# Softmax attention: the scores of the next two query tiles move from all five parts of a unit's output into its first two

## The chip, the cores and the metric

The kernel runs on one core of a Trainium2 chip. The metric is the device time of one execution in microseconds (µs). Its engines run side by side, each through its own list of instructions in order: TensorE (PE: matmuls; PEld: its weight loads), VectorE (DVE), ScalarE (ACT), GpSimd (POOL) and SyncE (SP, which issues transfers).

## The reference, cut to what matters

The whole kernel is a network of two blocks with two layers each; the change lies in the attention of its first layer. It has 6 query heads over 2 key heads, 1024 queries, and 256 + 1024 keys (a context and the sequence itself):

```python
def one_block(qblk):
    s = jnp.einsum('bqhgd,bkhd->bhgqk', qblk, k, preferred_element_type=jnp.float32) * scale
    p = jax.nn.softmax(s, axis=-1).astype(v.dtype)
    return jnp.einsum('bhgqk,bkhd->bqhgd', p, v)
...
y = jnp.concatenate([ya * jax.nn.silu(a_gate), yb * jax.nn.silu(b_gate)], axis=-1)
```

## The kernel before, in words

Every product of two fp32 operands is made of three matmuls of rounded parts (`mm3`, lines 202 to 204): a value x is split into a high part h and a low part l, and h·h, h·l, l·h are added up in PSUM. A split (`split`, lines 215 and 216) is a cast on ScalarE, which gives h, and a subtraction on VectorE, which gives l.

The attention (`ev_attn`) works in 24 **units**, numbered 0 to 23 here: head h = unit // 4, and in it pair pr = unit % 4 of two query tiles of 128 rows, **a** and **b**. What a unit needs is made in two generators.

`scores`, for each of the two tiles: matmuls into `pss` (6 of 512 columns, the sequence's keys; the pool has two such buffers) and into one half of `psc` (3 of 256 columns, the context's keys). Then the softmax: two maxima on VectorE (L602 over psc, L603 over pss), the bias from them (L604, L605), two exponentials on ScalarE with their sums (L608 gives `em`, L609 gives `ec`), and on VectorE the sum and its reciprocal (L610, L611). It has four steps: scores a, softmax a, scores b, softmax b.

`output`, in five parts. The weights of both tiles are transposed on TensorE in five **turns** T0 to T4 of four 128x128 blocks each (L627 into `pt`; T0 reads ec, T1 to T4 read em). Each turn is split into `pT`. Five **products** P0 to P4 of 6 matmuls (256 columns) add pT times the values up in `po`, where a small transpose also spreads the reciprocals (L649). Part 1 is T0 and T1; part 2 is L649, P0, T2; part 3 is P1; part 4 is T3, P2, T4, P3; part 5 is P4 and the gating on VectorE (L664, then L666 for heads 0 to 2, or L671 and one more split for heads 3 to 5).

The loop over units runs the `output` of unit n and, between its parts, the `scores` of unit n+1. At a unit's end `self.go()` now and then adds a piece of other work, the preparation of a later layer (**side work**, many small VectorE instructions, `s5_prep`).

This text is not the order on the engines. A scheduler takes it as a priority list, models when each instruction could start, and writes a fixed order for each engine; buffers are handed out on the way. An engine then executes its list in order and stops at the first instruction whose wait is not met. `pt`, `po` and `psc` share four buffers, `pss` has two.

Of the kernel before, what the change touches and what calls it, by code (L numbers as in the profile page):

```python
# [103 lines left out]
class Core:  # L104
# [468 lines left out]
    def ev_attn(self, ks, vs, scls):  # L573
# [5 lines left out]
        def head(h):  # L579
            qh, ql = self.tr("qh"), self.tr("ql")  # L580
            nc.sync.dma_start(qh.bitcast(F32), self.q_d[h, 0])
            nc.sync.dma_start(ql.bitcast(F32), self.q_d[h, 1])
            bg = self.t("bgl")
            nc.sync.dma_start(bg, self.bg_d[h])
            heads[h] = qh, ql, scls[h], bg

        def scores(h, pr, es):
            qh, ql, scl, _ = heads[h]
            kh, kl, kch, kcl = ks[h // 3]
            pc = self.psb("psc")  # L590
            for i in range(2):
                qt = 2 * pr + i
                qc = slice(qt * P, (qt + 1) * P)
                ps = self.psB("pss")
                cc = slice(i * CTX, (i + 1) * CTX)
                self.mm3(pc[:, cc], qh[:, qc], ql[:, qc], kch, kcl, True, True)
                for hv in HALVES:
                    self.mm3(ps[:, hv], qh[:, qc], ql[:, qc], kh[:, hv], kl[:, hv], True, True)
                yield
                st = self.s("st", [P, 8], "st", 6)  # L600
                sq = scl[:, qt:qt + 1]
                nc.vector.tensor_reduce(st[:, 1:2], pc[:, cc], axis=AX.X, op=ALU.max)  # L602
                nc.vector.tensor_reduce(st[:, 0:1], ps, axis=AX.X, op=ALU.max)  # L603
                nc.vector.tensor_scalar(st[:, 3:4], st[:, 0:1], st[:, 1:2], -1.0, op0=ALU.max, op1=ALU.mult)  # L604
                nc.vector.tensor_tensor(st[:, 3:4], st[:, 3:4], sq, op=ALU.mult)  # L605
                em = self.t("em")
                ec = self.s("ec", [P, CTX], "s1", 5)
                nc.scalar.activation(em, ps, AF.Exp, bias=st[:, 3:4], scale=sq, accum_out=st[:, 4:5])  # L608
                nc.scalar.activation(ec, pc[:, cc], AF.Exp, bias=st[:, 3:4], scale=sq, accum_out=st[:, 5:6])  # L609
                nc.vector.tensor_tensor(st[:, 6:7], st[:, 4:5], st[:, 5:6], op=ALU.add)  # L610
                nc.vector.reciprocal(st[:, 7:8], st[:, 6:7])  # L611
                es.append((ec, em, st))
                yield

        def output(h, pr, es):
            dc = slice((h // 3) * P, (h // 3 + 1) * P)
            pts = {}

            def weights_t(g):
                pt = self.psb("pt")  # L620
                for j in range(2):
                    kt = 2 * g + j
                    for i in range(2):
                        ec, em, _ = es[i]
                        src = ec[:, kt * P:(kt + 1) * P] if kt < 2 else em[:, (kt - 2) * P:(kt - 1) * P]
                        o = (2 * j + i) * P
                        nc.tensor.transpose(pt[:, o:o + P], src, self.ident)  # L627
                pT = self.tr("pT", (P, 2, HB))
                self.split(pt, pT[:, 0], pT[:, 1])
                pts[g] = pT  # L630

            def product(g):
                pT = pts.pop(g)
                for j in range(2):
                    kt = 2 * g + j
                    if kt < 2:
                        vh, vl = vC[:, 0, kt, dc], vC[:, 1, kt, dc]
                    else:
                        tt = kt - 2
                        vh, vl = vH[tt // 4][:, tt % 4, dc], vL[tt // 4][:, tt % 4, dc]  # L640
                    c2 = slice(j * CTX, (j + 1) * CTX)
                    self.mm3(po[:, :CTX], vh, vl, pT[:, 0, c2], pT[:, 1, c2], kt == 0, kt == 9)

            weights_t(0)
            weights_t(1)
            yield
            po = self.psb("po")
            for i in range(2):
                nc.tensor.matmul(po[:, CTX + i * P:CTX + i * P + P], es[i][2][:, 7:8].to_broadcast([P, P]), self.ident,  # L649
                                 start=True, stop=True)  # L650
            product(0)
            weights_t(2)
            yield
            product(1)
            yield
            weights_t(3)
            product(2)
            weights_t(4)
            product(3)
            yield  # L660
            product(4)
            cs = slice(pr * CTX, (pr + 1) * CTX)
            gate = self.s("gate", [P, CTX], "s1", 5)
            nc.vector.tensor_tensor(gate, po[:, CTX:], heads[h][3][:, cs], op=ALU.mult)  # L664
            if h < 3:
                nc.vector.tensor_tensor(y[2 + h][:, cs], po[:, :CTX], gate, op=ALU.mult)  # L666
                if pr == 3:
                    nc.gpsimd.dma_start(self.y_d[2 + h], y[2 + h])
            else:
                yo = self.s("yo", [P, CTX], "s1", 5)  # L670
                nc.vector.tensor_tensor(yo, po[:, :CTX], gate, op=ALU.mult)  # L671
                self.split(yo, y[2 + h][0][:, cs], y[2 + h][1][:, cs])
# [6 lines left out]
        for n, (h, pr) in enumerate(units):  # L679
            if pr == 0:  # L680
                y[2 + h] = self.t("yf") if h < 3 else (self.tr("yh"), self.tr("yl"))
            if pr == 2 and h < 5:
                head(h + 1)
            nxt = []
            sc = scores(*units[n + 1], nxt) if n + 1 < len(units) else iter(())
            o = output(h, pr, es)
            next(o)
            next(sc, None)
            next(o)
            next(sc, None)  # L690
            next(o)
            next(sc, None)
            next(o)
            next(sc, None)
            next(o, None)
            es = nxt
            self.go()
# [1520 lines left out]
```

## Time and profile before

| | |
|---|---|
| time, median of 3 runs | 4103.86 µs (4103.34 to 4109.02) |
| the profiled execution's own time | 4098.59 µs |
| its span (first to last instruction) | 4096.8 µs |
| PE, PEld, DVE, ACT busy over the span | 93%, 77%, 69%, 35% |
| attention: start of the first scores, start of the last gating (L671) | 533.5 and 817.7 µs |
| end of unit 0's first turns, about; start of unit 23's L664 | 546.70; 817.19 µs |
| mean from one L664 to the next | 11.3 µs |

The execution that was profiled took 4098.59 µs, 1.8 µs more than its span. The attention is one fourteenth of the span. "Busy" of PE counts from the start of a matmul to its modelled end; matmuls overlap, so a busy PE may still be short of work.

### The profile page before, as it was taken

The numbers are of one execution on the slowest core, as the hardware profiler recorded it, in microseconds if no ns is written. First come the engines' busy times: TensorE is split into PE (matmuls) and PEld (weight loads), VectorE is DVE, ScalarE is ACT, GpSimd is POOL, SyncE is SP. The second block draws the span as 40 slices with busy tenths as digits, with TensorE's granted clock in tenths as the row PEclk, the third lists the DMA queues.
The fourth block names the chain that finished last, engine by engine and source line by source line (L and its number), as shares of the span: only waits on it lengthen the run. The fifth ranks groups of instructions, "written<-read, shape, count | busy, mean of one in ns | idle before, by whom it ended". The sixth has DMA issues, their size and how long they took to land.

```text
span 4096.8 us, 51285 instructions
## 1 busy us (share of the span) xinstructions
PE 3816.4 (93%) x19684; PEld 3148.8 (77%) x19684; DVE 2842.5 (69%) x4892; ACT 1446.9 (35%) x2328; POOL 304.0 (7%) x533
## 2 busy tenths in 40 slices
PE   6899998899999996899999999989999899999997
PEld 3787887778788876687788888768787677888886
DVE  5676667785889787767866654457888867666544
ACT  3222245532112221434432333245555534232332
POOL 0001100041010022000000000010010000000000
PEclk9999999999999998999999999989999999999998
DMA  5434321163122348423322245333232333222542
GB/s 208 135 127 147 106 73 42 53 202 118 67 83 74 106 150 260 131 67 108 113 83 80 75 162 174 100 95 91 73 98 73 98 119 113 78 77 97 172 146 100
DMA packets 172907, 458.35 MB, mean 112 GB/s; under 512 B 38542, under 2 KB 59028, under 8 KB 172662
## 3 DMA queue, kind: packets, MB, share of 16 engines
q1 hardware_dynamic: 129254, 317.94, 23.5%
q0 software_dynamic: 41104, 132.41, 9.7%
q10 hardware_dynamic: 2304, 4.72, 0.3%
q8 instruction: 155, 2.54, 0.3%
q14 instruction: 90, 0.74, 0.1%
HBM read 327.07 MB, written 100.66 MB: 104 GB/s over the span
## 4 chain that ended last, share of the span: by engine, by line
PE 72%; DVE 11%; issue 4%; ACT 3%; DMA 2%; POOL 1%; SPq 1%; DVEq 0%; ACTq 0%; POOLq 0%
PE p L202 7%; PE p L203 7%; PE p L204 7%; PE pd L202 4%; PE pd L203 4%; PE pd L204 4%; PE pout L202 2%; PE pout L204 2%; PE pout L203 2%; PE pu L202 2%; PE pu L204 2%; PE pu L203 2%; DVE sbm L1946 2%; PE pwt L1967 1%; PE pz L1041 1%
## 5 line engine op out<-in xcount | busy, mean ns | idle before, releaser
L185 DVE TENSOR_TENSOR wl<-wt,wh 128x1024 fp32r<-128x1024 f32 x232 | 283.5, 1223 | 316.5 <-ACT wh L184 315.0
L184 ACT CAST wh<-wt 128x1024 fp32r<-128x1024 f32 x232 | 243.5, 1050 | 728.3 <-PE pd L203 218.6
L202 PE MATMUL p<-tq,wq 128*128 128x512 f32 x736 | 291.7, 396 | 3.5 <-ACT wq L215 3.5
L203 PE MATMUL p<-tq,wq 128*128 128x512 f32 x736 | 290.9, 395 | 0.0
L204 PE MATMUL p<-tq,wq 128*128 128x512 f32 x736 | 290.4, 395 | 0.0
L202 PE MATMUL pd<-hd,wh 128*128 128x512 f32 x704 | 278.7, 396 | 0.0
L203 PE MATMUL pd<-hd,wh 128*128 128x512 f32 x704 | 278.5, 396 | 0.0
L204 PE MATMUL pd<-hd,wl 128*128 128x512 f32 x704 | 278.3, 395 | 0.0
L204 PE MATMUL p<-hq,wq 128*128 128x512 f32 x480 | 189.9, 396 | 0.0
L203 PE MATMUL p<-hq,wq 128*128 128x512 f32 x480 | 189.6, 395 | 0.0
L202 PE MATMUL p<-hq,wq 128*128 128x512 f32 x480 | 189.5, 395 | 0.0
L215 ACT CAST wq<-ws 128x512 fp32r<-128x512 f32 x184 | 114.4, 623 | 209.5 <-PE p L204 204.9
L1717 DVE TENSOR_TENSOR fsg<-fsg,p 128x512 f32<-128x512 f32 x140 | 94.4, 686 | 117.9 <-PE p L204 117.9
L202 PEld LDWEIGHTS p<-tq,wq 128*128 128x128 f32 x736 | 138.1, 188 | 43.9 <-ACT wq L215 4.8
L204 PEld LDWEIGHTS p<-tq,wq 128*128 128x128 f32 x736 | 138.3, 188 | 33.1
L203 PEld LDWEIGHTS p<-tq,wq 128*128 128x128 f32 x736 | 138.3, 188 | 31.1
L1717 DVE TENSOR_TENSOR fsu<-fsu,p 128x512 f32<-128x512 f32 x140 | 94.5, 687 | 94.9 <-PE p L204 94.9
L216 DVE TENSOR_TENSOR wq<-ws,wq 128x512 fp32r<-128x512 f32 x184 | 126.7, 690 | 47.4 <-ACT wq L215 45.0
L204 PEld LDWEIGHTS pd<-hd,wl 128*128 128x128 f32 x704 | 132.3, 188 | 32.1
L202 PEld LDWEIGHTS pd<-hd,wh 128*128 128x128 f32 x704 | 132.2, 188 | 32.1
L203 PEld LDWEIGHTS pd<-hd,wh 128*128 128x128 f32 x704 | 132.2, 188 | 31.9
L202 PE MATMUL pu<-hq,wh 128*128 128x512 f32 x320 | 129.9, 406 | 9.4 <-DVE cv L978 9.4
(702 smaller groups left out, 10668.3 us busy)
## 6 DMA issues: line engine op xcount, KB each, us to landing
wt<-w_gu SPq DMA_DIRECT2D x88, 512.0 KB
wt<-w_dn SPq DMA_DIRECT2D x88, 512.0 KB
wm<-w_mod SPq DMA_DIRECT2D x48, 512.0 KB
hid<-fsg POOLq DMA_DIRECT2D x44, 512.0 KB, 3.9
hr<-hid SPq DMA_DIRECT2D x44, 512.0 KB
wt<-w_od SPq DMA_DIRECT2D x28, 512.0 KB
khat<-fX POOLq DMA_DIRECT2D x24, 512.0 KB, 3.0
kh<-khat SPq DMA_DIRECT2D x24, 512.0 KB
```

Source lines behind the costliest of these rows:

```text
L184: nc.scalar.copy(wh, wt)
L185: nc.vector.tensor_tensor(wl, wt, wh.bitcast(F32), op=ALU.subtract)
L202: mm(ps, lh, rh, start=first, stop=False)
L203: mm(ps, lh, rl, start=False, stop=False)
L204: mm(ps, ll, rh, start=False, stop=last)
L215: self.nc.scalar.copy(h, src)
L216: self.nc.vector.tensor_tensor(l, src, h.bitcast(F32), op=ALU.subtract)
L1041: mm(p4[:, i, q], tb[:, m], z[:, self.POS[m]], start=True, stop=False)
L1717: add = lambda o, u, v: tt(o, u, v, op=ALU.add)
L1946: nc.vector.tensor_tensor_scan(om[:, :n - 1], om[:, :n - 1], self.inv[:, 3:4].to_broadcast([P, n - 1]), 1.0, op0=ALU.mult, op1=ALU.add)
L1967: nc.tensor.transpose(pt[:, s * P:(s + 1) * P], W[x][:, c:c + P], self.ident)
```

## The change

Only the order in which the loop asks the two generators for their next step:

```diff
             sc = scores(*units[n + 1], nxt) if n + 1 < len(units) else iter(())
             o = output(h, pr, es)
+            next(sc, None)
             next(o)
+            next(sc, None)
             next(sc, None)
             next(o)
             next(sc, None)
             next(o)
-            next(sc, None)
             next(o)
-            next(sc, None)
             next(o, None)
             es = nxt
             self.go()
```

Before: part 1, scores a, part 2, softmax a, part 3, scores b, part 4, softmax b, part 5. Now: scores a, part 1, softmax a, scores b, part 2, softmax b, parts 3 to 5. No instruction is added or removed, but the scheduler is given another list, and the engines' orders differ from the start of the attention to its end (on PE, DVE and ACT; those of POOL and SP are the same). After the attention all orders are the same as before.

ScalarE, in the output of unit 4 (the casts of T0 to T4, and the exponentials of unit 5: em and ec of its tile a, then of b). Before:

```order
L215 CAST pT_4384<-pt_4379 128x512
L215 CAST pT_4392<-pt_4387 128x512
L215 CAST pT_4420<-pt_4415 128x512
L608 ACTIVATE em_4428,st_4423<-pss_4396,st_4423,qscl1_2472 128x1024
L609 ACTIVATE ec_4429,st_4423<-psc_4395,st_4423,qscl1_2472 128x256
L215 CAST pT_4455<-pt_4450 128x512
L215 CAST pT_4469<-pt_4464 128x512
L608 ACTIVATE em_4483,st_4478<-pss_4440,st_4478,qscl1_2472 128x1024
L609 ACTIVATE ec_4484,st_4478<-psc_4395,st_4478,qscl1_2472 128x256
```

Now, the same unit:

```order
L215 CAST pT_4395<-pt_4390 128x512
L215 CAST pT_4403<-pt_4398 128x512
L608 ACTIVATE em_4411,st_4406<-pss_4380,st_4406,qscl1_2472 128x1024
L609 ACTIVATE ec_4412,st_4406<-psc_4379,st_4406,qscl1_2472 128x256
L215 CAST pT_4441<-pt_4436 128x512
L608 ACTIVATE em_4449,st_4444<-pss_4417,st_4444,qscl1_2472 128x1024
L609 ACTIVATE ec_4450,st_4444<-psc_4379,st_4444,qscl1_2472 128x256
L215 CAST pT_4466<-pt_4461 128x512
L215 CAST pT_4480<-pt_4475 128x512
```

Tile b's exponentials stood behind the casts of T3 and T4, last in the unit; now they stand ahead of them, and tile a's stand ahead of the cast of T2.

VectorE, from the first subtraction of unit 4 (pT of T0, T1 and T2; st_4406 and st_4423 belong to unit 5's tile a, st_4444 to its tile b; yf is unit 3's gating). Before:

```order
L216 TENSOR_TENSOR pT_4384<-pt_4379,pT_4384 128x512
L216 TENSOR_TENSOR pT_4392<-pt_4387,pT_4392 128x512
L602 TENSOR_REDUCE st_4423<-psc_4395 128x1
L604 TENSOR_SCALAR st_4423<-st_4423 128x1
L605 TENSOR_TENSOR st_4423<-st_4423,qscl1_2472 128x1
L216 TENSOR_TENSOR pT_4420<-pt_4415,pT_4420 128x512
```

Now:

```order
L216 TENSOR_TENSOR pT_4395<-pt_4390,pT_4395 128x512
L666 TENSOR_TENSOR yf_3889<-po_4301,gate_4369 128x256
L216 TENSOR_TENSOR pT_4403<-pt_4398,pT_4403 128x512
L604 TENSOR_SCALAR st_4406<-st_4406 128x1
L605 TENSOR_TENSOR st_4406<-st_4406,qscl1_2472 128x1
L610 TENSOR_TENSOR st_4406<-st_4406 128x1
L611 RECIPROCAL st_4406<-st_4406 128x1
L216 TENSOR_TENSOR pT_4441<-pt_4436,pT_4441 128x512
L602 TENSOR_REDUCE st_4444<-psc_4379 128x1
L604 TENSOR_SCALAR st_4444<-st_4444 128x1
L605 TENSOR_TENSOR st_4444<-st_4444,qscl1_2472 128x1
L603 TENSOR_REDUCE st_4525<-pss_4499 128x1
```

L602 and L603 of tile a now come earlier (in the output of unit 3). Between the bias of tile a and that of tile b stand L610 and L611, which wait for tile a's exponentials, and the subtraction of T2.

TensorE, with what an instruction waits for, at the place where one unit's turns give way to the next. Before, the end of unit 4 and the turns T0 (pt_4498) and T1 (pt_4506) of unit 5, whose tile b is em_4483 and ec_4484:

```order
L627 MATMUL pt_4506<-ident_63,em_4428 128x128 [waits PE_49]
L203 MATMUL pss_4515<-kl_3378,qh_4128 128x512
L204 MATMUL pss_4515<-kh_3377,ql_4129 128x512
L627 MATMUL pt_4506<-ident_63,em_4483 128x128 [waits Activation_49]
L627 MATMUL pt_4506<-ident_63,em_4428 128x128
```

Now, in unit 4 behind turn T4 (pt_4475). pss_4499 and pss_4536 are the scores of unit 6, tiles a and b; pss_4536 takes the buffer of pss_4417, which em_4449 above reads:

```order
L627 MATMUL pt_4475<-ident_63,em_4285 128x128 [waits PE_49]
L627 MATMUL pt_4475<-ident_63,em_4323 128x128
L627 MATMUL pt_4475<-ident_63,em_4285 128x128
L627 MATMUL pt_4475<-ident_63,em_4323 128x128
L204 MATMUL pss_4499<-kh_3377,ql_4129 128x512
L202 MATMUL pss_4536<-kh_3377,qh_4128 128x512 [waits Activation_49]
L203 MATMUL pss_4536<-kl_3378,qh_4128 128x512
L204 MATMUL pss_4536<-kh_3377,ql_4129 128x512
L202 MATMUL psc_4498<-kc_916,qh_4128 128x256 [waits Activation_49]
L203 MATMUL psc_4498<-kc_916,qh_4128 128x256
L204 MATMUL psc_4498<-kc_916,ql_4129 128x256
L202 MATMUL po_4427<-pT_4466,vH_918 128x256 [waits Activation_49]
```

Before, the next unit's turns wait for the exponential of tile b. Now they have it long before, and it is the scores two units ahead that wait for it, with P3 and P4 of the running unit queued behind them.

## Rows read from the trace of the kernel before

**Rows 1.** Stretches from one L664 to the next: busy time by engine, granted clock, DMA.

```profile
core 0: us, PE busy (x) PEld busy (x) DVE busy (x) ACT busy (x) POOL busy (x), PEclk, DMA share, GB/s
...
632.06:645.91 13.85, 10.78 (x73) 9.14 (x72) 13.78 (x74) 6.44 (x16) 0.53 (x1) 1.00 0.25 100
...
667.11:678.00 10.89, 9.42 (x71) 8.84 (x71) 6.93 (x20) 7.16 (x14) 0.00 (x0) 1.00 0.29 84
...
723.79:739.15 15.36, 11.96 (x73) 10.43 (x72) 12.66 (x45) 5.66 (x14) 0.00 (x0) 0.89 0.27 100
...
771.57:786.65 15.08, 12.53 (x74) 10.42 (x72) 11.66 (x26) 5.53 (x14) 0.00 (x0) 0.89 0.00 1
...
808.39:817.19 8.80, 7.79 (x57) 6.77 (x57) 6.33 (x25) 4.27 (x10) 0.00 (x0) 1.00 0.72 270
817.19:826.00 8.81, 8.05 (x34) 5.92 (x33) 8.81 (x36) 5.15 (x6) 0.00 (x0) 1.00 0.61 231
sum 279.30, PE 254.27 PEld 222.91 DVE 216.91 ACT 156.41 POOL 1.60; mean PE 10.17 PEld 8.92 DVE 8.68 ACT 6.26 POOL 0.06
```

**Rows 2.** What TensorE's weight loads waited for, 533 to 820 µs: total, times, longest.

```profile
PEld pt L627 <- ACT em L608: 20.2, 18, 2.6
PEld pss L202 <- ACT em L608: 12.4, 8, 5.5
PEld po L203 <- DVE pT L216: 10.3, 23, 1.4
```

**Rows 3.** Timeline of TensorE in one unit: start, duration, instruction, idle before it.

```profile
659.66 0.60 PE L627 MATMUL pt<-ident,em 128*128 128x128 f32 x4
...
660.22 0.28 PE L203 MATMUL po<-pT,vH 128*128 128x256 f32 x1
...
661.67 0.39 PE L203 MATMUL po<-pT,vH 128*128 128x256 f32 x1
...
663.12 0.50 PE L202 MATMUL pss<-kh,qh 128*128 128x512 f32 x1 [0.16 <-ACT em L608]
...
663.69 0.40 PE L204 MATMUL pss<-kh,ql 128*128 128x512 f32 x1
663.93 0.28 PE L202 MATMUL psc<-kc,qh 128*128 128x256 f32 x1
664.04 0.28 PE L203 MATMUL psc<-kc,qh 128*128 128x256 f32 x1
...
668.58 0.55 PE L627 MATMUL pt<-ident,em 128*128 128x128 f32 x3 [1.79 <-ACT em L608]
```

**Rows 4.** Timeline of ScalarE in the same unit.

```profile
660.30 0.59 ACT L215 CAST pT<-pt 128x512 fp32r<-128x512 f32 x1 [2.03 <-PE pt L627]
...
662.97 0.56 ACT L609 ACTIVATE ec<-psc,st,qscl 128x256 f32<-128x256 f32 x1
...
663.51 1.07 ACT L215 CAST pT<-pt 128x512 fp32r<-128x512 f32 x2
667.23 1.21 ACT L608 ACTIVATE em<-pss,st,qscl 128x1024 f32<-128x1024 f32 x1 [2.65 <-DVE st L605]
```

**Rows 5.** Timeline of VectorE in the same unit.

```profile
658.00 1.28 DVE L216 TENSOR_TENSOR pT<-pt,pT 128x512 fp32r<-128x512 f32 x2
...
660.92 0.69 DVE L216 TENSOR_TENSOR pT<-pt,pT 128x512 fp32r<-128x512 f32 x1 [0.39 <-ACT pT L215]
...
663.65 0.16 DVE L610 TENSOR_TENSOR st<-st 128x1 f32<-128x1 f32 x1 [1.97 <-ACT ec L609]
...
665.33 0.41 DVE L602 TENSOR_REDUCE st<-psc 128x1 f32<-128x256 f32 x1
665.66 1.22 DVE L603 TENSOR_REDUCE st<-pss 128x1 f32<-128x1024 f32 x1
666.79 0.21 DVE L604 TENSOR_SCALAR st<-st 128x1 f32<-128x1 f32 x1
667.03 0.16 DVE L605 TENSOR_TENSOR st<-st,qscl 128x1 f32<-128x1 f32 x1
```

## The prediction

> **What bounds the kernel now.** I read the page first: PE is busy 93% of the span, and the attention is one stretch where it is less so. Then the stretches from one L664 to the next, which cut the attention into its units [rows 1]. From 546.70 µs, with the first turns of unit 0 done, to unit 23's L664 there are 279.30 − 8.81 = 270.49 µs for 24 units, 11.27 each. Three stretches, with much more VectorE work (13.78, 12.66 and 11.66 µs against 6.93 in a clean one), carry side work; they take 13.85, 15.36 and 15.08. The other 21 take (270.49 − 44.29) / 21 = 10.77 on average, so side work costs 44.29 − 3 × 10.77 = 12.0 µs. What does a unit's matmul work need? A turn takes 660.22 − 659.66 less one matmul, about 0.45; a 256-column matmul 0.12, a 512-column one 0.23 [rows 3]. Five turns (2.25), L649 (0.45), 30 + 6 matmuls of 256 (4.2) and 12 of 512 (2.8) make 9.7. So the units lie about 1 µs above their matmuls, and TensorE is not the only bound.
>
> The waits say what the rest is [rows 2]: turns wait for em, 20.2 µs in all, scores for em (their buffer) 12.4, products for the subtraction 10.3. And the timeline of one unit shows the loop: turn T2 at 659.66, its cast at 660.30, subtraction at 660.92, and so on through ScalarE and VectorE, em at 667.23, and the next turns at 668.58 after 1.79 of idling [rows 3 to 5]. One chain through three engines, not the matmuls, sets the unit.
>
> **The change, part by part.** No instruction comes or goes; SP and POOL have the same lists. So the sum is that of 24 units in the new orders, times the rows' durations. I take these steps from the rows: turn to cast 0.64 (659.66 to 660.30), cast 0.59, two in a row 1.07, subtraction 0.03 later, 0.69, the next 0.60 behind it; subtraction to product 0.06 (661.61 to 661.67); L602 0.41 and 0.33 to the next instruction, L603 1.22 and 1.13 to the next; L604 0.24, L605 0.20 until em starts; em 1.21, 0.14 until TensorE has its buffer (0.10 assumed after ec); ec to L610 0.68, ec to the next cast 0.54 [rows 3 to 5].
>
> *Removed.* The turns' wait for em (20.2 µs): b's exponentials now stand in the middle of the unit before, and T0 finds them done.
>
> *Added.* The lists of unit 4 (shown above) run like this, from its T0 at t = 0. Casts of T0, T1: 0.64 to 1.72. Subtraction T0 1.26 to 1.95; then yf, subtraction T1 from 2.2 to 2.9, and only then L604 at 2.80 and L605 for tile a: em a 3.24 to 4.45, ec a to 5.0. L610 and L611 wait for them (5.12, 5.32). Cast of T2 4.98 to 5.57, subtraction 5.60 to 6.29; only then L602 b at 6.2, L604, L605: em b 7.08 to 8.29, ec b to 8.84, casts of T3, T4 8.82 to 9.90. On TensorE: T0, T1 to 0.90; L649 takes T0's buffer and waits until 2.01; P0, T2, P1, T3 to 4.76; scores a (their buffer came free at 4.59), context scores b, P2 to 6.97; T4 and a's last matmul to 7.65. Here it stops: scores b of two units ahead need em b's buffer, so 8.43. Three matmuls, the context's, one of P3 and three more take it to 10.28, the rest of P3 and P4 to 11.57, where the next T0 starts. The unit takes **11.6 µs**, of which TensorE stands 1.9: 1.1 at L649, 0.8 at scores b.
>
> What is queued behind that last wait is P3, P4, the next T0 and with it the next round of the same chain: nothing hides it, since each engine's next link stands in order behind the one before. That is the cost of putting softmax b into the middle: its em sits ahead of the casts of T3 and T4, and its bias behind T2's subtraction.
>
> The other orders, by the same steps. **A**, as above: 9 units (2 to 4, 6 to 8, 10 to 12), 11.6 each. **C**: units 0, 1, 5, 9, where L604 and L605 of tile a stand ahead of T0's subtraction, so em a starts at 1.7 with the casts done; the scores of the next unit are not yet asked for at T3; 11.0 each. **A′**: units 15, 16, 19, 20 of heads 3 to 5, with the extra split of yo ahead of L604 a (em a 0.35 later) and L603 of the next tile a, 1.13, between L602 b and L604 b: em b 8.56 to 9.77, scores b at 9.91, 13.1 each. **B1**: 13, 17, 21, with ec a and the split of yo ahead of the casts of T0 and T1, so P0 gets its operand at 4.1, but the scores of tile b are left for the next unit: 11.1. **B2**: 14, 18, with both L603 in the chain and six 512-column matmuls ahead of L649: em a 4.43, em b 9.41 to 10.62, 13.9. Units 22 and 23, with less or no softmax left, 11.6 and as before 8.8 [rows 1].
>
> Sum: 9 × 11.6 + 4 × 11.0 + 4 × 13.1 + 3 × 11.1 + 2 × 13.9 + 11.6 + 8.8 = 282.3 µs. Side work comes on top. From below it is hidden: between L605 and L610 VectorE waits for two exponentials anyway (1.97 of idling in the row [rows 5]), and about half of the pieces stand there. From above it costs its 12.0 as before. I take 10, nearer to the upper end, since the other half stands ahead of an L604 or of a subtraction, in the chain. That makes 292.3 against 270.5: **+21.8 µs**, so 4098.6 + 21.8 = 4120.4 for an execution like the profiled one. The median of the runs shown lies 5.3 above that execution; on it the forecast is 4125.7. I say 4124.
>
> How far can the sum be off? Each order's chain has about 25 links; 0.4 µs per unit either way is 8.8 over 22 units, and side work from hidden to 12 adds −10 or +2. So +3 to +33 on top of 4098.6 to 4103.9: 4102 to 4137.
>
> **A rule on headroom.** By matmul busy time the units have 279.30 − 254.27 = 25 µs left, by weight loads 279.30 − 222.91 = 56 [rows 1]. The Trainium skill, "Trainium Kernel Development and Optimization", Best Practices, says that the distance to the limit is judged by weight loads, not by matmul busy time. By that the change would have up to 56 µs to win; but a 512-column matmul takes longer than its load, and the count above, 24 × 9.7 = 233, leaves 270.5 − 233 = 37.
>
> **Rivals.**
>
> *Faster: the wait at the turns simply goes.* For it: it is the largest wait [rows 2], and T0 no longer needs anything late. If the chain had slack, 20.2 µs of weight-load idling would go, up to 37 at the matmul bound: about 4080, and 4062 at most. Against it: T0's wait ends on a chain, and the new orders don't shorten that chain but close it elsewhere. It decides in this way if em b in A is done before TensorE comes to scores b, at 7.65: em b would have to start 0.8 earlier than 7.08.
>
> *No change: one wait for another.* If L604, L605 and the subtractions take less of VectorE than I count (0.8 µs per unit), the units come out at 10.8 to 11.3, as before: 4100 to 4108.
>
> *Slower still: the clock.* In the stretches with the longest waits (up to 5.5 µs [rows 2]) the granted clock is 0.89, in those with waits of 1.8 it is 1.00 [rows 1, 3]. If the 2.1 µs that A′ waits at scores b took the clock to 0.89 in A′ and B2, it would cost 0.11 × 13.5 × 6 = 9 µs more: 4135. The Trainium skill, "TensorE: Matmul & The Clock Gate", A second HAM failure mode, says that frequent short idling between matmul groups can make the clock go back and forth; the stretch at 667.11 with its 1.79 wait does not show that.
>
> **How the numbers follow.** Of no change a measurement of this kernel can tell about 0.2%, 8 µs. The chain as worked out (beyond +8): 0.74; the clock on top of it: 0.03; no change within 8: 0.13; faster: 0.10. So slower 0.77, same 0.13, faster 0.10. The likeliest case's own range is 4112 to 4140; taking in half of the case of no change, 4106 to 4140 holds 8 in 10.
>
> **What would show it.** In the profile after: turns waiting for em, 20.2 µs before, nearly nothing; the scores' wait for em 12.4 before, 20 to 40; L649 waiting for a subtraction, some 10 to 20. Casts of T3 after ec b, em a after the subtraction of T1. Stretches from L664 to L664 of 11.6 in units 2 to 7 with little scatter, 13 to 14 in the A′ and B2 units; the time up to 540 µs and from 830 µs on unchanged. It is wrong if stretches of A are at 10.5 or less, or if scores find their buffers free.

## The result, and the profile after

| | before | after |
|---|---|---|
| median of the runs | 4103.6 µs (4102.3 to 4109.02, 4 runs) | 4133.77 µs (4127.42 to 4134.88, 4 runs) |
| ratio, 95% interval | | 1.0069 (1.0055 to 1.0084) |
| the profiled execution (its span) | 4098.59 (4096.8) µs | 4127.42 (4125.6) µs |
| first to last L664 (units 0 to 23) | 259.76 µs | 285.42 µs |

The change makes the kernel 0.7% slower. Of the 28.8 µs between the two profiled executions, 25.5 are there at the last L664 (842.71 against 817.19 µs). Behind it the orders are the same and the distance wanders (the last L978, in the next layer, starts at 1357.3 against 1333.6, 23.7 later); executions of the kernel before alone lie up to 14.1 µs apart (4095.1 to 4109.24 in 13 runs). The remaining 3.3 µs are therefore not put down to the change.

The stretches from one L664 to the next, as in [rows 1]. The first is a unit of kind C, the second of kind A (kinds as in the prediction); then a B1 and a B2, an A′ with side work, the other B2, and unit 22:

```profile
core 0: us, PE busy (x) PEld busy (x) DVE busy (x) ACT busy (x) POOL busy (x), PEclk, DMA share, GB/s
557.29:568.22 10.93, 10.41 (x75) 9.20 (x74) 7.79 (x21) 6.18 (x13) 0.00 (x0) 1.00 0.16 53
...
591.44:603.14 11.70, 10.22 (x74) 9.16 (x73) 8.14 (x20) 6.20 (x13) 0.53 (x1) 1.00 0.11 46
...
697.47:707.49 10.02, 8.49 (x62) 7.59 (x61) 6.01 (x19) 6.41 (x14) 0.00 (x0) 1.00 0.01 2
707.49:722.48 14.99, 12.46 (x85) 11.04 (x84) 10.68 (x23) 6.50 (x14) 0.00 (x0) 1.00 0.00 1
...
735.51:752.86 17.35, 12.66 (x76) 10.89 (x75) 13.44 (x49) 6.50 (x14) 0.00 (x0) 0.90 0.26 92
...
762.89:779.25 16.36, 13.86 (x83) 12.25 (x82) 10.85 (x23) 6.50 (x14) 0.00 (x0) 0.90 0.00 1
...
820.29:834.98 14.69, 11.89 (x72) 10.45 (x71) 8.76 (x21) 7.08 (x15) 0.00 (x0) 0.83 0.10 31
```

Before, the stretches of units 1 to 12 without side work scattered between 8.23 and 12.09 µs; now the eight units of kind A without side work lie between 11.52 and 11.94. What TensorE's weight loads waited for in the attention (533 to 846 µs), as in [rows 2]:

```profile
PEld pss L202 <- ACT em L608: 31.1, 22, 4.9
PEld po L203 <- DVE pT L216: 12.4, 17, 2.6
PEld po L649 <- DVE pT L216: 12.1, 10, 1.3
...
PEld pt L627 <- ACT em L608: 0.4, 1, 0.4
```

The wait that the change takes away is gone (20.2 µs before, 0.4 now); the scores' wait for their buffer and a new one of L649 have taken its place. One unit of kind A, from its T0 at 591.05, shows how. VectorE, as in [rows 5]:

```profile
592.30 0.69 DVE L216 TENSOR_TENSOR pT<-pt,pT 128x512 fp32r<-128x512 f32 x1 [0.45 <-ACT pT L215]
592.91 0.41 DVE L666 TENSOR_TENSOR yf<-po,gate 128x256 f32<-128x256 f32 x1
593.24 0.68 DVE L216 TENSOR_TENSOR pT<-pt,pT 128x512 fp32r<-128x512 f32 x1
593.84 0.20 DVE L604 TENSOR_SCALAR st<-st 128x1 f32<-128x1 f32 x1
594.08 0.16 DVE L605 TENSOR_TENSOR st<-st,qscl 128x1 f32<-128x1 f32 x1
596.15 0.16 DVE L610 TENSOR_TENSOR st<-st 128x1 f32<-128x1 f32 x1 [1.91 <-ACT ec L609]
...
596.63 0.69 DVE L216 TENSOR_TENSOR pT<-pt,pT 128x512 fp32r<-128x512 f32 x1
597.23 0.42 DVE L602 TENSOR_REDUCE st<-psc 128x1 f32<-128x256 f32 x1
597.68 0.21 DVE L604 TENSOR_SCALAR st<-st 128x1 f32<-128x1 f32 x1
```

ScalarE, as in [rows 4]: em of tile a, the cast of T2, em of tile b, the casts of T3 and T4.

```profile
594.27 1.20 ACT L608 ACTIVATE em<-pss,st,qscl 128x1024 f32<-128x1024 f32 x1 [1.51 <-DVE st L605]
...
596.01 0.58 ACT L215 CAST pT<-pt 128x512 fp32r<-128x512 f32 x1
598.13 1.20 ACT L608 ACTIVATE em<-pss,st,qscl 128x1024 f32<-128x1024 f32 x1 [1.53 <-DVE st L605]
...
599.87 1.07 ACT L215 CAST pT<-pt 128x512 fp32r<-128x512 f32 x2
```

TensorE, as in [rows 3]: L649, the scores of tile b, the next unit's T0.

```profile
593.05 0.71 PE L649 MATMUL po<-ident,st 128*128 128x128 f32 x4 [0.96 <-DVE pT L216]
...
599.48 0.50 PE L202 MATMUL pss<-kh,qh 128*128 128x512 f32 x1 [0.52 <-ACT em L608]
...
602.74 0.60 PE L627 MATMUL pt<-ident,ec 128*128 128x128 f32 x4
```

Read together, these rows form one closed round. Tile a's bias stands behind the subtraction of T1, so em a starts 3.22 µs behind T0. The cast of T2 and L610 come only when tile a's exponentials are done; behind them come the subtraction of T2 and tile b's bias, and em b at 7.08. The scores follow at 8.43 and the next T0 at 11.69. TensorE stands only 1.5 µs in it, and still the unit is 0.9 longer than the average one without side work before. In the profile's own chain, the work that ended last followed back, this round stands whole in five of the nine units of kind A (2, 3, 6, 10 and 11). In the other four, the one shown among them, that chain runs over the subtraction of T0, L649, the matmuls and L603 of the next tile, or over the side work: a second path, of about the same length.

### The profile page after: what moved, and what is told of

It is laid out like the page before. It is cut to its first block, busy times and chain, and to the rows that moved or that the text cites. A ratio compares the mean times of both kernels' runs of the same rounds, so it can differ in the third digit from the quotient of the medians.

```text
span 4125.6 us, 51294 instructions
## 1 busy us (share of the span) xinstructions
PE 3821.3 (93%) x19684; PEld 3152.5 (76%) x19684; DVE 2842.1 (69%) x4892; ACT 1442.0 (35%) x2328; POOL 303.2 (7%) x533
## 4 chain that ended last, share of the span: by engine, by line
PE 76%; DVE 13%; issue 4%; ACT 3%; DMA 3%; POOL 1%; SPq 1%; DVEq 0%; ACTq 0%; POOLq 0%
PE p L202 7%; PE p L204 7%; PE p L203 7%; PE pd L202 4%; PE pd L204 4%; PE pd L203 4%; PE pout L202 2%; PE pout L204 2%; PE pout L203 2%; DVE sbm L1946 2%; PE pu L202 2%; PE pu L204 2%; PE pu L203 2%; PE pwt L1967 1%; PE pz L1041 1%
## 5 line engine op out<-in xcount | busy, mean ns | idle before, releaser
L202 PE MATMUL p<-tq,wq 128*128 128x512 f32 x736 | 292.3, 397 | 3.5 <-ACT wq L215 3.5
L203 PEld LDWEIGHTS p<-tq,wq 128*128 128x128 f32 x736 | 138.6, 188 | 31.1
L215 ACT CAST wq<-wt 128x512 fp32r<-128x512 f32 x138 | 85.3, 618 | 150.0 <-PE p L204 145.3
```

Source lines behind the costliest of these rows:

```text
L202: mm(ps, lh, rh, start=first, stop=False)
L203: mm(ps, lh, rl, start=False, stop=False)
L215: self.nc.scalar.copy(h, src)
```

## The experiments

Two theories. **The chain**: the fixed lists of VectorE and ScalarE close a round through em a, the cast and subtraction of T2, em b and the scores, and its length is the unit's. **The buffers**: the unit is long because the scores are asked for before one of their two buffers is free, which is where TensorE waits longest. "Stage" below is the time from the first L664 to the last in the profiled execution; the first L664 itself starts at 557.4 before and between 553.3 (runs 2 and 9) and 560.8 (runs 1 and 6) elsewhere, so up to 4 µs of a difference lie ahead of the stage. "Given high priority" means that the scheduler picks the instruction ahead of others that could start. The kernel before was run again beside each group: runs 1 to 4 are compared with its first median, 5 to 8 with the second, 9 with the third.

| kernel | stage, µs | median, µs (runs, or lowest to highest) | ratio to before, 95% |
|---|---|---|---|
| before | 259.76 | 4104.14 (25), 4101.84 (13), 4102.22 (9) | 1 |
| the change | 285.42 | 4133.77 (4) | 1.0069 (1.0055 to 1.0084) |
| 1: before, softmax b ahead of part 4 | 331.92 | 4176.75 (4171.62 to 4180.66) | 1.0181 (1.0166 to 1.0196) |
| 2: the change, softmax b last | 259.00 | 4095.80 (10) | 0.9988 (0.9979 to 0.9998) |
| 3: the change, bias first | 263.16 | 4101.60 (10) | 0.9995 (0.9986 to 1.0005) |
| 4: as 3, context scores together | 252.18 | 4095.72 (10) | 0.9983 (0.9974 to 0.9993) |
| 5: the change, context scores together | 277.53 | 4117.13 (6) | 1.0034 (1.0022 to 1.0046) |
| 6: the change, longer bias | 316.28 | 4149.70 (4) | 1.0119 (1.0102 to 1.0135) |
| 7: softmax b last, context scores together, maxima and bias first | 240.20 | 4076.12 (6) | 0.9936 (0.9923 to 0.9949) |
| 8: scores b behind part 2, context scores together, bias first | 243.28 | 4081.95 (6) | 0.9950 (0.9936 to 0.9963) |
| 9: before, context scores together, bias first | 237.35 | 4077.83 (5) | 0.9944 (0.9931 to 0.9958) |

**1. Only softmax b moved**, from behind part 4 to ahead of it; the scores stay where they were in the kernel before.

```diff
             next(o)
             next(sc, None)
-            next(o)
             next(sc, None)
+            next(o)
             next(o, None)
```

> The order before with one step moved: softmax b stands ahead of part 4 of the output, its scores stay where they were (output, scores a, output, softmax a, output, scores b, softmax b, output, output). Theory (one chain through the lists of ScalarE and VectorE): em b ahead of the casts of T3 and T4, and the two L603 in the chain; steps by the rows give 13 to 14 us per unit, so slower than the change itself: 4140 to 4165. Rival (the scores wait for their two buffers because they are asked for too early): the scores are late here and the turns no longer wait for em b, so the wait at the turns (20 us) goes and none takes its place: 4070 to 4095.

It is the slowest of all, beyond the chain's range and on the other side of before from that of the buffers. Two of its stretches from L664 to L664:

```profile
576.64:588.89 12.25, 10.84 (x75) 9.34 (x74) 8.46 (x21) 6.21 (x13) 0.00 (x0) 1.00 0.01 1
588.89:603.85 14.96, 11.95 (x73) 10.42 (x72) 8.25 (x20) 6.41 (x13) 0.00 (x0) 0.89 0.32 106
```

And the wait for the scores' buffer:

```profile
PEld pss L202 <- ACT em L608: 63.0, 32, 5.5
```

The scores are asked for late, and wait longer than in any other run: asking for them early is not what makes them wait. The chain's range left out the clock: 14 of the 23 stretches have a granted clock of 0.80 to 0.92, as the second row has, against 5 of 23 in the change. That this makes up the excess over the range is not shown.

**2. The change with softmax b put back to the end**: scores a and b and softmax a stay early.

```diff
             next(sc, None)
             next(o)
-            next(sc, None)
             next(o)
             next(o)
+            next(sc, None)
             next(o, None)
```

> The change with softmax b left at the end, between parts 4 and 5 (scores a, output, softmax a, scores b, output, output, output, softmax b, output). Theory (chain): the casts of T3 and T4 stand ahead of em b again; units alternate between some 10 and 13 us, mean 11.2 to 11.6 with side work: 4100 to 4118, most of the loss gone. Rival (buffers): both scores are asked for early and the buffers are held longer than in the change: 4130 or more.

All of the loss is gone, and a little more than the chain foresaw; with units of 11.4 and 10.7 µs in turn:

```profile
575.58:586.96 11.38, 11.18 (x76) 9.69 (x74) 9.17 (x21) 4.79 (x10) 0.00 (x0) 1.00 0.29 90
586.96:597.62 10.66, 9.71 (x70) 8.78 (x70) 7.10 (x19) 7.86 (x17) 0.53 (x1) 1.00 0.25 103
```

Yet the wait at the buffers is nearly that of the change:

```profile
PEld pss L202 <- ACT em L608: 26.9, 21, 4.9
```

(In every order one such wait, of 4.2 to 5.5 µs, lies ahead of unit 0's turns; it is in these sums.) What has gone instead are the waits of L649, 12.1 µs for subtractions of pT and 5.3 for the gating (L666 and L671) in the change and none here. So asking early for the scores costs nothing by itself. It is softmax b in the middle of the unit that costs, in the lists that come of it.

**3. The change with L604 and L605 given high priority**, for both tiles, so that tile a's bias stands ahead of the subtractions of T0 and T1, and tile b's ahead of that of T2.

```diff
-                nc.vector.tensor_scalar(st[:, 3:4], st[:, 0:1], st[:, 1:2], -1.0, op0=ALU.max, op1=ALU.mult)
-                nc.vector.tensor_tensor(st[:, 3:4], st[:, 3:4], sq, op=ALU.mult)
+                with self.tc.high_priority(): nc.vector.tensor_scalar(st[:, 3:4], st[:, 0:1], st[:, 1:2], -1.0, op0=ALU.max, op1=ALU.mult)
+                with self.tc.high_priority(): nc.vector.tensor_tensor(st[:, 3:4], st[:, 3:4], sq, op=ALU.mult)
```

> The change, with the bias of each tile (L604, L605) given high priority, so that on VectorE it stands ahead of the subtractions of T0 and T1 (tile a) or of T2 (tile b); ScalarE keeps the change's order. Theory (chain): em a starts at 1.7 instead of 3.2 us into the unit, as in the units of kind C: units of A at 10.8 to 11.1 instead of 11.65, those of heads 3 to 5 shorter by 0.5 to 1; 4112 to 4125. Rival (buffers): the scores are asked for at the same places, so as the change, 4127 to 4137.

```profile
587.05 0.20 DVE L604 TENSOR_SCALAR st<-st 128x1 f32<-128x1 f32 x1
...
587.50 0.15 DVE L605 TENSOR_TENSOR st<-st,qscl 128x1 f32<-128x1 f32 x1
587.73 0.69 DVE L216 TENSOR_TENSOR pT<-pt,pT 128x512 fp32r<-128x512 f32 x1
```

Em a now starts at 588.07, as soon as the casts of T0 and T1 are done, and the whole loss goes, with all steps of the change in place: more than the 4112 to 4125 that the chain promised. The orders moved elsewhere too. Units now take about 12.5 and 9.2 in turn, the long ones with more of the matmuls (PE busy 12.5 and 8.2), and in this short one em b starts 3.5 µs behind em a, at 591.55, where it was 3.9 in the unit of the change shown above. The wait at the buffers fell with the time, from 31.1 to this:

```profile
PEld pss L202 <- ACT em L608: 13.7, 7, 4.9
```

So this run refutes the time that the buffers forecast, but does not tell the two theories apart by the wait; run 2 does.

**4. As 3, and the context scores of both tiles asked for together with tile a's**, into the two halves of psc, so that L602 of tile b no longer waits for three matmuls behind ec a.

```diff
-                self.mm3(pc[:, cc], qh[:, qc], ql[:, qc], kch, kcl, True, True)
+                if i == 0: [self.mm3(pc[:, t * CTX:(t + 1) * CTX], qh[:, (qt + t) * P:(qt + t + 1) * P], ql[:, (qt + t) * P:(qt + t + 1) * P], kch, kcl, True, True) for t in range(2)]
```

> As e3, and the context scores of tile b (3 matmuls) are issued with those of tile a, so that they don't wait for ec a, which reads the same PSUM tile. Theory (chain): the link ec a, context scores b, L602 b goes too; em b starts soon after ec a: units of A at 10.1 to 10.6; 4098 to 4115. Rival (buffers): as the change, 4127 to 4137.

Another 6 µs, and a time just below before; the gain that the chain forecast was again too small.

**5. The context scores alone**, without priority (the diff of 4 on top of the change).

> The change, with the context scores of both tiles asked for together with tile a's (nine matmuls of 256 columns in a row into both halves of psc); no priorities. It takes one link out of the chain: L602 of tile b no longer waits until tile a's ec and three matmuls are done, and stands ahead of the subtraction of T2 instead of between it and L604 b. The bias of tile a still stands behind the subtraction of T1. Chain: em b comes about 0.4 us earlier in the units of kind A and A-prime, so 13 x 0.4 = 5 us less than the change, 4125 to 4132. Rival (it is the context link that makes the change slow, the place of tile a's bias costs nothing): most of the loss goes, 4100 to 4112.

Between the two forecasts. In the stage, units 1 to 12 gained nothing (140.71 µs from the first L664 to unit 12's, 140.18 in the change), against the 0.4 per unit expected; the 8 µs came from the units behind, most of them from those that are of kind A′ in the change (13.03 to 10.48 µs and 13.66 to 10.61 without side work). VectorE in a unit of kind A whose T0 is at 591.07 shows why:

```profile
596.24 0.42 DVE L602 TENSOR_REDUCE st<-psc 128x1 f32<-128x256 f32 x1
...
597.25 0.20 DVE L604 TENSOR_SCALAR st<-st 128x1 f32<-128x1 f32 x1
597.62 1.23 DVE L603 TENSOR_REDUCE st<-pss 128x1 f32<-128x1024 f32 x1 [0.17 <-PE pss L204]
598.76 0.15 DVE L605 TENSOR_TENSOR st<-st,qscl 128x1 f32<-128x1 f32 x1
```

L602 is a µs earlier than in the change, but the scheduler then put L603 of the next tile a, 1.23 µs, between the two instructions of tile b's bias: em b starts 7.88 µs behind T0 instead of 7.08.

**6. A longer bias**: in the change, L605's value is copied twice more on VectorE.

```diff
-                nc.vector.tensor_tensor(st[:, 3:4], st[:, 3:4], sq, op=ALU.mult)
+                nc.vector.tensor_tensor(st[:, 3:4], st[:, 3:4], sq, op=ALU.mult); nc.vector.tensor_scalar(st[:, 2:3], st[:, 3:4], 1.0, None, op0=ALU.mult); nc.vector.tensor_scalar(st[:, 3:4], st[:, 2:3], 1.0, None, op0=ALU.mult)
```

> The change, with two more small VectorE instructions in each tile's bias behind L605 (its value is copied twice, about 0.2 us each with the step to the next), so that em starts some 0.45 us later; the orders of ScalarE stay the same in the units of kind A. Chain: tile a's 0.45 and tile b's 0.45 both lie in the loop of a kind-A unit, since tile b's bias stands behind L610 and L611, which wait for tile a's exponentials: 0.5 to 0.9 more per unit, 22 units, 4145 to 4155. Rival (the bias has slack, and the units are long because TensorE is asked for the scores before their buffers are free or runs at a lower clock): 46 x 0.45 us of VectorE work lies in its idle time, 4130 to 4138.

The median is on the chain's side. The profiled execution is the slowest of the four (4159.47 µs, the others 4144.11 to 4154.78), and 8 of its 23 stretches have a granted clock of 0.78 to 0.90, against 5 in the change, so its stage overstates the loss; the unit read here has 1.00. It lost a µs more than I had expected, since the lists changed again. In the unit of kind A whose T0 is at 601.94:

```profile
608.50 0.42 DVE L602 TENSOR_REDUCE st<-psc 128x1 f32<-128x256 f32 x1
609.04 1.23 DVE L603 TENSOR_REDUCE st<-pss 128x1 f32<-128x1024 f32 x1
610.18 0.20 DVE L604 TENSOR_SCALAR st<-st 128x1 f32<-128x1 f32 x1
...
612.34 0.50 PE L202 MATMUL pss<-kh,qh 128*128 128x512 f32 x1 [2.30 <-ACT em L608]
```

L603 of the next tile a has come between L602 and L604 of tile b again, and L604 starts 1.68 µs behind L602, 0.45 in the change. So em a starts 3.60 µs behind T0 (0.38 later than in the change) and em b, at 610.99, 9.05 behind it: 1.97 later, of which the copies of both tiles make 0.76 and L603 1.23. The next T0 comes 13.66 behind this one, 11.69 in the change: 1.97 as well. All of em b's lateness is in this unit's length. In kind C (the unit from 616.01) em b is 1.6 µs later by the same comparison and the unit grew from 10.95 to 11.69: there the scores had their buffer before and wait 0.86 now, so half of the lateness was covered.

**7. Softmax b last as in 2, the context scores as in 4, and L602 to L605 given high priority** (beside the diffs of 2 to 4):

```diff
-                nc.vector.tensor_reduce(st[:, 1:2], pc[:, cc], axis=AX.X, op=ALU.max)
-                nc.vector.tensor_reduce(st[:, 0:1], ps, axis=AX.X, op=ALU.max)
+                with self.tc.high_priority(): nc.vector.tensor_reduce(st[:, 1:2], pc[:, cc], axis=AX.X, op=ALU.max)
+                with self.tc.high_priority(): nc.vector.tensor_reduce(st[:, 0:1], ps, axis=AX.X, op=ALU.max)
```

> Tile b's softmax asked for last in the unit, as in the second run of the study, with the context scores of both tiles together with tile a's, and L602 to L605 given high priority in the scheduler, so that the maxima and the bias stand ahead of the subtractions. Chain: the two exponentials lie half a unit apart, neither behind a subtraction; no turn and no scores wait for long, and a unit comes to 9.9 to 10.6 us instead of 11.3: 4075 to 4092, faster than before. Rival (the units are bound by something that these orders don't touch, buffers or the clock): as the two runs that it joins, 4093 to 4104.

In the chain's range, 0.6% faster than the kernel before and 1.4% faster than the change. The wait at the scores is down to 6.4 µs in four places, 4.3 of them ahead of unit 0. Two of its stretches:

```profile
573.60:583.98 10.38, 10.38 (x75) 9.58 (x74) 7.89 (x21) 6.36 (x13) 0.00 (x0) 1.00 0.34 99
583.98:593.51 9.53, 9.53 (x71) 8.90 (x70) 7.97 (x21) 6.33 (x13) 0.53 (x1) 1.00 0.28 115
```

TensorE is busy for the whole of each of these two: here the matmuls are the bound, close to the 9.7 per unit counted in the prediction.

**8. Scores b behind part 2**: the order scores a, part 1, softmax a, part 2, scores b, parts 3 and 4, softmax b, part 5, with the context scores as in 4 and the priority as in 3.

```diff
             next(o)
             next(sc, None)
-            next(sc, None)
             next(o)
             next(sc, None)
             next(o)
             next(o)
+            next(sc, None)
             next(o, None)
```

> The steps in the order scores a, part 1, softmax a, part 2, scores b, parts 3 and 4, softmax b, part 5 (tile b's scores behind part 2 instead of ahead of it), with the context scores of both tiles together with tile a's and L604 and L605 given high priority in the scheduler. Chain: as the run beside it, but tile b's scores are asked for only when their buffer is about to be free: units of 9.9 to 10.6, 4078 to 4094. Rival (bound by something that these orders don't touch): 4093 to 4104.

In the chain's range too.

**9. The kernel before, untouched in its steps, with the two edits of 4.**

> The kernel before, its steps in their own order (part 1, scores a, part 2, softmax a, part 3, scores b, part 4, softmax b, part 5), with the context scores of both tiles asked for together with tile a's, and L604 and L605 given high priority in the scheduler: what the two fastest runs share, without the change's earlier steps. Chain: L602 b no longer waits for three matmuls behind ec a, which takes some 0.4 us off in some units, but em b still stands behind the split of T3 and the next unit's T0 still waits for it: 4088 to 4100. Rival (the context scores and the priority alone made those runs fast, the order of the steps does not matter): 4072 to 4086.

The rival's time is right and my own forecast was wrong. Without any step moved it is as fast as 7. What TensorE's weight loads waited for:

```profile
PEld pss L202 <- ACT em L608: 9.9, 3, 5.2
...
PEld pt L627 <- ACT em L608: 5.0, 17, 0.6
```

The timeline of one unit, L605 of tile b, the subtraction of T3, and em b:

```profile
599.04 0.15 DVE L605 TENSOR_TENSOR st<-st,qscl 128x1 f32<-128x1 f32 x1
...
599.44 0.69 DVE L216 TENSOR_TENSOR pT<-pt,pT 128x512 fp32r<-128x512 f32 x1
...
600.33 1.22 ACT L608 ACTIVATE em<-pss,st,qscl 128x1024 f32<-128x1024 f32 x1
```

And the sum over its stretches from L664 to L664:

```profile
sum 237.35, PE 229.22 PEld 205.63 DVE 195.41 ACT 144.76 POOL 1.60; mean PE 9.97 PEld 8.94 DVE 8.50 ACT 6.29 POOL 0.07
```

I had taken it that em b's bias comes behind the split of T3, whatever the priority, as long as softmax b is asked for behind part 4. It now stands ahead of T3's subtraction, em b follows the cast of T4 without a wait (2.65 before [rows 4]), and starts 3.2 µs behind the cast of T2 (at 597.14) instead of 6.9 [rows 4]. So the turns wait 5.0 µs in all instead of 20.2. The two edits take 24 µs off the kernel before and 38 off the change (4133.77 to 4095.72); the change costs 30 µs without them and still 18 with them. So the order of the steps does matter: what the rival says of it holds for runs 7 to 9, not for run 4.

## Why the prediction was right

The sign and the mechanism were right. The size, 21.8 µs forecast between profiled executions and 28.8 measured, was a quarter too small, and 4133.77 lies 10 µs above the 4124 named. By its own steps:

- **Removed.** The turns' wait for em: 20.2 to 0.4, as said.
- **Kind A.** Of the steps worked out for it, L649 starts 2.00 µs behind T0 (forecast 2.01), em a at 3.22 (3.24), em b at 7.08 (7.08), scores b at 8.43 (8.43), the next T0 at 11.69 (11.57). Only the wait at scores b is 0.52 instead of 0.8, since one more 512-column matmul stands ahead of it than I counted. The eight units without side work sum up to 93.5 µs, forecast 92.8.
- **C, B1, A′.** The four C (unit 0 from 546.70) take 43.7, forecast 44.0. B1 and B2 are right only as a pair: 10.02 + 14.99 = 25.0 for units 13 and 14, forecast 11.1 + 13.9 = 25.0; L664 falls earlier than I drew it, so the sign of 13 to 14 µs for B2 missed (14.99 and 16.36). The two A′ without side work take 13.03 and 13.66, forecast 13.1.
- **Side work.** 17.35 − 13.1, twice, and 13.61 − 11.6: 10.5 in all, forecast 10. The clock is in it: both stretches of 17.35 have a granted clock of 0.90, as the two before had 0.89 [rows 1].
- **The term that was too small** is the stage: 842.71 − 546.70 = 296.0 against 292.3. Of the 3.7, 1.4 lie in units 17 and 18, 1.0 in 21 to 23, 0.6 in unit 19, 0.5 in side work; the rest is spread. The first of these is the clock, part of the rival that I had given 0.03: stretches of the same order without side work take 14.99 at a granted clock of 1.00 and 16.36 at 0.90. In 21 to 23 it is likely: units 22 and 23 have 0.83 and 0.89 now and 1.00 before, but no stretch of their order at 1.00 shows what it costs. That the median lies near that rival's 4135 is chance, since the clock did not fall in unit 14 or in the units of kind A′ without side work.
- **Beyond the stage.** 28.8 − 25.5 = 3.3 between the two profiled executions, and another 1.3 between the medians' distance of 30.2 and 28.8, within what executions of one kernel scatter.

The prediction read one row wrongly. It ties the granted clock of 0.89 to the longest waits, up to 5.5 µs [rows 2]. That wait ends at 541.58 µs, ahead of unit 0. The longest waits of weight loads in the two stretches at 0.89 are 3.22 and 1.59 µs, while a wait of 2.59 in another stretch left the clock at 1.00 [rows 1, from 632.06]:

```profile
734.05 0.29 PEld L202 LDWEIGHTS pss<-kh,qh 128*128 128x128 f32 x1 [3.22 <-ACT em L608]
...
781.50 0.19 PEld L202 LDWEIGHTS pss<-kh,qh 128*128 128x128 f32 x1 [1.59 <-ACT em L608]
```

So the length of the longest wait does not tell where the clock falls.

The rivals: that the wait simply goes fell with em b at 7.08. That L604, L605 and the subtractions take less than counted fell with the same rows (subtraction of T1 at 593.24, em a at 594.27, as worked out). The buffers, set up as a rival for the runs, fell by their times in runs 1 to 3; only in run 2 does the wait stay while the loss goes.

Where my reasons went too far is what lies behind the result. I had read "the order of the steps" as the cause; runs 3 and 9 show that what counts is where the scheduler then puts the tiles' biases, the exponentials and L603 in the lists. My sizes for what moving those brings were too small in runs 3, 4 and 9, and too large for units 1 to 12 in run 5; in run 5 another instruction, L603, had come in between. What stays open is how much of the gain in runs 3 and 4 comes from em a itself and how much from the scores and softmax that moved up with it, and what the 18 µs between runs 4 and 9 are made of: no run holds the rest of the lists fixed.

Of the room in the units, run 9, the one with the shortest stage, gained 22.4 µs (259.76 to 237.35) and then had TensorE busy for nearly all of it (229.22 of 237.35), with weight loads at 205.63. Of the 37 that the matmul count left and the 56 by weight loads, the smaller was nearer, as far as these orders show. The rule on headroom in the Trainium skill ("Trainium Kernel Development and Optimization", Best Practices) names, beside weight loads, the share of the peak that the matmul work reaches (MFU), which the prediction left out.

## What to carry to other kernels

When a scheduler turns a priority list into fixed orders, read the new lists and walk one round of them with durations from the old trace: here that gave the new length of the commonest unit to 0.1 µs. The largest wait need not be what makes a round long (run 2); look also for the small instruction that a long exponential waits for (here two of 0.2 µs each, behind a subtraction) and try putting that first. Check each edit's whole list afterwards, since a 1.2 µs maximum that slips into the gap can give the gain back (run 5).

## What was unexpected of the hardware

The granted clock did not follow from the order alone. Units 14 and 18 have the same order and, within 0.04 µs, the same waits, and the clock fell in one of them; the scores of tile b in unit 14 and in unit 18, and a 512-column matmul 1.3 and 1.5 µs behind them:

```profile
718.81 0.50 PE L202 MATMUL pss<-kh,qh 128*128 128x512 f32 x1 [1.93 <-ACT em L608]
...
720.07 0.40 PE L202 MATMUL pss<-kh,qh 128*128 128x512 f32 x1
...
774.23 0.50 PE L202 MATMUL pss<-kh,qh 128*128 128x512 f32 x1 [1.94 <-ACT em L608]
...
775.71 0.63 PE L202 MATMUL pss<-kh,qh 128*128 128x512 f32 x1
```

In unit 18 the granted clock is 1.00 up to 775 µs, 0.50 (the 1.2 GHz level) between 776 and 778, when TensorE had been busy again since 774.23, and 1.00 from 779; the matmul takes 0.63 µs instead of 0.40, and the stretch 1.4 more. What differed between the two units before the fall, the trace does not show. "TensorE: Matmul & The Clock Gate", A second HAM failure mode, in the Trainium skill speaks of a clock that goes back and forth when short idling is frequent: unit 18 agrees, unit 14 with the same idling does not.
